# Splitting every tile of probabilities into two rounded parts, with one PSUM bank for the accumulator of values

## The chip, the cores and the metric

The kernel runs on one core of a Trainium2 chip. The metric is the device time of one execution in microseconds (us). The engines are named as in the profile: PE (matrix multiplication; PEld loads its weights), DVE (VectorE), ACT (ScalarE), POOL (GpSimd), SP (the queue that issues the DMAs). PSUM has eight banks of 128 x 512 float32 that PE writes and that ACT and DVE read.

## What is computed

One decoder layer for 1024 tokens of width 1024: attention beside a short convolution, then a gated feed-forward part, then a gated embedding. The change lies in the attention. For a block of 128 queries t (0 to 7) and a group g of four heads, three softmaxes are taken over different keys, and each is multiplied with its own values:

```
p_c = masked_softmax(s_c, cmp_end[None, :] <= tq[:, None])        # 63 compressed blocks
o_c = jnp.einsum('bgrqn,bngd->bqgrd', p_c, vcmp)
o_s = jnp.einsum('bgrqnk,bgqnkd->bqgrd', p_s, v_sel)              # selected keys (here all earlier ones)
o_w = jnp.einsum('bgrqk,bkgd->bqgrd', p_w, vwb)                   # a window of 512 keys
return gb[..., 0:1] * o_c + gb[..., 1:2] * o_s + gb[..., 2:3] * o_w
```

Behind it follow a norm over the heads and the product with w_o, whose rows feed the feed-forward part.

## The kernel before

Most products are taken in fp32r, a rounded float32, with both factors split into a rounded part and a remainder (high and low), so that three products stand for one. The values here hold high and low side by side in 128 columns, so a tile of probabilities needs two products: one for its high part `ph`, one for its low part `pl`.

The attention is written as 16 **units** (t, g), t from 7 down to 0, in slots: `at(slot, rank, fn)` files a piece of work under a slot and a rank, `run` carries them out in that order, and inside `tc.manual_schedule()` the instructions of each engine stand in the order in which they were recorded. While the scores of one unit are made (`score`: PE L666 to L669, DVE maximum L677, ACT exponential L683, DVE reciprocal L692, POOL scaling L694), `values` handles the tiles of the unit before it. For each tile of 128 keys:

- `turn`: PE transposes the four heads' probabilities into one PSUM bank (L719, tile `ba`);
- `keep`: ACT rounds the bank into `ph` (L731), and a slot part later DVE computes `pl` = bank minus `ph` (L735);
- `weigh`: PE multiplies `ph` and `pl` into the unit's accumulator, 128 x 512 (L753). The first `pl` of a unit is kept for last and closes the sum (L758).

`PLAIN[t]` says which tiles are not split: ACT copies the bank as it is into `pf` (L727), DVE does nothing, and PE multiplies `pf` in plain float32, which takes two passes in the profile. There are 28 such tiles of 148: 4 in each unit of t=7, 2 in t=3, 3 in t=2, 3 in t=1, 2 in t=0, none in t=6 to 4.

At a unit's end `close` empties the accumulator: ACT copies the lower half (`pvlo`, L767) and DVE adds it to the upper one (`oT`, L771, two instructions). For g=1, `norm_heads` follows (ACT `osq`, `oh`; DVE `ol` L810; PE sums L817; POOL power; PE spread L165 and ACT `rab`).

The accumulator's tile is `bv`, of which two may be open at once. The banks 4 to 7 serve the accumulator and the transposes, the others the scores. After the slots the last pieces and the rows of w_o (`row`, PE L101 to L103, then `row_rest` and `keep_form`) stand outside the manual order, and the scheduler of the language decides where they go. The rows of the second half of the tokens (`oh1`) depend on t=4 to 7 alone.

Of the kernel before, what the change touches and what calls it, by code (L numbers as in the profile page):

```python
# [10 lines left out]
P = 128  # L11
# [9 lines left out]
NCMP = 64  # L21
EPS = 1e-6
NEG = -1e30
PLAIN = (2, 2, 2, 1, 0, 0, 0, 2)

F32 = _mybir.dt.float32
F32R = _mybir.dt.float32r
# [14 lines left out]
X = dict(cmode=0, cd_r=5.98, ad_s=0, ad_r=5.27, nh_r=7, cl_s=0, cl_r=3.2, keep_s=1, keep_r=2,   # L42
         low_s=0, low_r=3.5, w_s=1, w_r=2.9, turn_r=3, sc_r=5, pk_s=0, pk_r=8, ex_s=1, ex_r=4, scl_s=1,
         scl_r=1, root_s=2, root_r=2.6, ap_s=2, ap_r=2.6, qs=5, qs_r=4.7, qt_s=2, qt_r=0.46, v0=2, off=0.0,
         ppf=6, pph=7, ppl=4, offu=4.46, v0r=-1, rt_l=3, fl_r=9, rv_r=1.79, rt_s=0, rt_r=2.6, pvb=2, trb=3,
         late=14, xa=3)


def _emit(nc, tc, d, out, tap=lambda *a: None):
# [4 lines left out]
    def S(shape, dt, tag, bufs=1):  # L54
        n_[0] += 1
        return sb.tile(list(shape), dt, tag=tag, bufs=bufs, name=f"{tag}_{n_[0]}")

    def PS(tag, bufs, cols=512, dt=F32):
        n_[0] += 1
        return psp.tile([P, cols], dt, tag=tag, bufs=bufs, name=f"{tag}_{n_[0]}")  # L60
# [4 lines left out]
    def psa(dt=F32):  # L65
        return PS("ba", 3, 512, dt)

    def psb():
        return PS("bb", 1)

    act, dve, pool, pe = nc.scalar, nc.vector, nc.gpsimd, nc.tensor
# [25 lines left out]
    def f32(ap):  # L97
        return ap.bitcast(F32)
# [21 lines left out]
    ident, ones, mhalf = small["ident"], small["ones"], small["mhalf"]  # L120
# [68 lines left out]
    with tc.manual_schedule():  # L189
# [5 lines left out]
        for k in range(KC):  # L195
# [3 lines left out]
            g = small["g_mix"][:, k:k + 1]  # L199
# [83 lines left out]
    for j in range(4):  # L283
# [17 lines left out]
        t = S([P, T], F32, "t4", 4)  # L301
# [17 lines left out]
        g = small["g_conv"][:, j:j + 1]  # L319
# [242 lines left out]
    vs, vw = va[:, :, 0:2], va[:, :, 2:4]  # L562
    vc = kx[:, NCMP + T + P:].rearrange("p (g c) -> p g c", g=2)
# [19 lines left out]
    def spans(t):  # L583
        nsel, w0 = (t + 1) * P, max(0, t - 4)
        return nsel, w0, (t + 1 - w0) * P

    def psa_(dt=F32):
        return psa(dt) if X["trb"] == 3 else PS("bt", X["trb"], 512, dt)
# [6 lines left out]
    def at(slot, rank, fn):  # L595
        todo.setdefault(slot, []).append((rank, len(todo.get(slot, ())), fn))

    stacks, probs, oT, sums, between = {}, {}, {}, {}, []
# [101 lines left out]
    def values(u, slot, ns):  # L700

        t, g = units[u]
        nsel, w0, nwin = spans(t)

        sel = [(vs[:, i, g], NCMP + i * P, P, False) for i in range(t + 1)]
        win = [(vw[:, w0 + i, g], NCMP + nsel + i * P, P, i % 4 < PLAIN[t]) for i in range(t + 1 - w0)]
        win.append((vc[:, g], 0, P, PLAIN[t] > 0))
        n = len(sel) + len(win)
        tiles = []
        while sel or win:  # L710
            tiles.append(win.pop(0) if win and (not sel or len(win) * (t + 1) > len(sel) * (t + 2 - w0)) and tiles
                         else sel.pop(0))
        st = {}

        def turn(i, s):
            v, pc, k, plain = tiles[i]
            pt = psa_()
            for r in range(4):
                pe.transpose(pt[0:k, r * P:(r + 1) * P], probs[u, r][:, pc:pc + k], ident)  # L719

            def keep():
                s1 = s + X["keep_s"]
                s2 = s1 + X["low_s"]
                s3 = s2 + X["w_s"]
                if plain:
                    pf = S([P, 512], F32, "pf", X["ppf"])[0:k]
                    act.copy(pf, pt[0:k])  # L727
                    at(s2, X["low_r"], lambda: at(s3, X["w_r"], lambda: weigh(i, s3, pf)))
                    return
                ph = S([P, 512], F32R, "ph", X["pph"])[0:k]  # L730
                act.copy(ph, pt[0:k])  # L731

                def low():
                    pl = S([P, 512], F32R, "pl", X["ppl"])[0:k]
                    dve.tensor_sub(pl, pt[0:k], f32(ph))  # L735
                    at(s3, X["w_r"], lambda: weigh(i, s3, ph, pl))
                at(s2, X["low_r"], low)
            at(s + X["keep_s"], X["keep_r"], keep)

        st["left"] = n  # L740

        def weigh(i, s, *ps):
            if "pv" not in st:
                st["pv"] = psb() if X["pvb"] == 1 else PS("bv", X["pvb"])
            pv, v = st["pv"], tiles[i][0]
            if len(ps) == 2 and "low" not in st:
                st["low"] = v, ps[1]
                ps = ps[0:1]
                first = True
            else:  # L750
                first = False
            for p in ps:
                pe.matmul(pv, f32(v) if tiles[i][3] else v, p, start=first, stop=False)  # L753
                if between:
                    between.pop(0)[1](s)
            st["left"] -= 1
            if st["left"] == 0:
                pe.matmul(pv, *st["low"], start=False, stop=True)  # L758
                at(s + X["cl_s"], X["cl_r"], lambda: close(s + X["cl_s"]))

        def close(s):
            pv = st["pv"]
            if g == 0:
                oT[t] = S([P, 4, P], F32, "oT", 2)
            if X["cmode"] == 0:
                lo = S([64, 512], F32, "pvlo", 1)
                act.copy(lo, pv[64:128])  # L767

                def add():
                    for par in range(2):  # L770
                        dve.tensor_tensor(oT[t][par * 64:par * 64 + 64, 2 * g:2 * g + 2],  # L771
                                          pv[0:64].rearrange("p (a b q) -> p b a q", a=2, b=2)[:, par],
                                          lo.rearrange("p (a b q) -> p b a q", a=2, b=2)[:, par], op=OP.add)
                    if g == 1:
                        at(s + 1, X["nh_r"], lambda: norm_heads(t, s + 1))
            else:
                parts = S([64, 1024], F32, "pvparts", 1)
                act.copy(parts[:, 512:1024], pv[64:128])
                at(s, X["cd_r"], lambda: dve.tensor_copy(parts[:, 0:512], pv[0:64]))
                pp = parts.rearrange("p (z a b q) -> p b z a q", z=2, a=2, b=2)  # L780

                def add():
                    for par in range(2):
                        dve.tensor_tensor(oT[t][par * 64:par * 64 + 64, 2 * g:2 * g + 2],
                                          pp[:, par, 0], pp[:, par, 1], op=OP.add)
# [63 lines left out]
    for u in range(len(units)):  # L849
# [3 lines left out]
        for i in range(slots[u]):  # L853
            r, part = (i, 0) if slots[u] == 4 else (i // 2, i % 2)
# [8 lines left out]
    def load_h0(m, hf, after=None):  # L863
        hins[m, hf] = S([P, 512], F32, "hin", 3)
        load(hins[m, hf], h0[m][:, hf * 512:(hf + 1) * 512], after)
# [8 lines left out]
    def keep_form(nm, k, y):  # L874
        i = FORMS.index(nm)
        where = i < 2, k
        if where not in forms_:
            forms_[where] = S([P, 2 if i < 2 else 5, 2, 512], F32R, f"forms{i < 2:d}{k}")
        hi, lo = (forms_[where][:, i if i < 2 else i - 2, z] for z in range(2))
        act.copy(hi, y)  # L880
        dve.tensor_sub(lo, y, f32(hi))  # L881
        form[nm][k] = hi, lo

    def row(m, hf, ps):
        s = slice(hf * 512, (hf + 1) * 512)
        wh, wl = (w[:, m % 2 * 4:m % 2 * 4 + 4] for w in wo[m // 2])
        for k in range(4):
            mm3(ps, wh[:, k], wl[:, k], oh[hf][:, k], ol[hf][:, k], k == 0, k == 3)
# [55 lines left out]
    for m in range(KC):  # L944
        load_h0(m, 1, late)
        if m % 2 == 0:
            wo[m // 2] = weights(d["wo_att"][m // 2], 1024, k=8, after=late)
        ps = PS("bh", 3)
        row(m, 1, ps)
        row_rest(m, 1, ps)  # L950
        keep_form("b11" if m < 4 else "b21", m % 4, yf[m, 1])
# [149 lines left out]
    with tc.manual_schedule():  # L1101
        for m in (0, 4, 1, 5):
            load_h0(m, 0)
        for n in range(-AHEAD, len(order)):
            if n >= 0:
                w, i = order[n]
# [87 lines left out]
    for k in range(KC):  # L1194
        hi = S([P, T], F32R, f"fh{k}")
        lo = S([P, T], F32R, f"fl{k}")
        g = small["g_ple"][:, k:k + 1]
# [22 lines left out]
    for m in range(KC):  # L1220
        wh, wl = wpg.pop() if wpg else weights(d["w_pg"][m], 1024, k=KC, by_act=True)
        for c, w in ((0, 512), (512, 512)) if m < KC - 1 else ((0, 512), (512, 256), (768, 256)):
            s = slice(c, c + w)
            ps = psa()[:, 0:w]
# [113 lines left out]
```

## Time and profile before

| | |
|---|---|
| median of 3 runs | 1489.8 us (1489.61 to 1490.05) |
| profiled execution | 1490.71 us, its span 1488.9 us |
| PE busy | 1433.8 us (96%) |
| DVE, ACT, POOL busy | 990.5, 584.2, 492.6 us |
| attention's units (values) | 358.5 to 612.2 us of the span |

Busy time of PE includes modelled ends of pipelined matmuls, so two neighbours overlap in it; the distance from one start to the next says what a matmul costs in a stream. The granted clock (PEclk) is 1.0 at 2.4 GHz and 0.5 at 1.2 GHz.

### The profile page before, as it was taken

The numbers are of one execution on the slowest core, as the hardware profiler recorded it, in microseconds if no ns is written. First come the engines' busy times: TensorE is split into PE (matmuls) and PEld (weight loads), VectorE is DVE, ScalarE is ACT, GpSimd is POOL, SyncE is SP. The second block draws the span as 40 slices with busy tenths as digits, with TensorE's granted clock in tenths as the row PEclk, the third lists the DMA queues.
The fourth block names the chain that finished last, engine by engine and source line by source line (L and its number), as shares of the span: only waits on it lengthen the run. The fifth ranks groups of instructions, "written<-read, shape, count | busy, mean of one in ns | idle before, by whom it ended". The sixth has DMA issues, their size and how long they took to land.

```text
span 1488.9 us, 19441 instructions
## 1 busy us (share of the span) xinstructions
PE 1433.8 (96%) x7207; PEld 1168.9 (79%) x7207; DVE 990.5 (67%) x1588; ACT 584.2 (39%) x1190; POOL 492.6 (33%) x467
## 2 busy tenths in 40 slices
PE   7999999998999999986999999999999999997998
PEld 6787898996777777765888888888888888876887
DVE  7645566546778888777777777877774344469533
ACT  4110131237868889653323333233335112125211
POOL 3221242465445558245223333333310000474000
PEclk9999999999989999997999999999999999999999
DMA  6221214300000002241222222222235123341211
GB/s 250 82 71 56 75 58 155 104 1 1 1 1 1 1 1 86 93 149 63 72 74 68 71 85 85 86 86 85 78 114 184 57 106 114 103 160 69 71 43 43
DMA packets 48190, 115.50 MB, mean 78 GB/s; under 512 B 5472, under 2 KB 8160, under 8 KB 48096
## 3 DMA queue, kind: packets, MB, share of 16 engines
q1 hardware_dynamic: 48096, 114.26, 22.8%
q8 instruction: 57, 0.93, 0.3%
q14 instruction: 37, 0.30, 0.1%
HBM read 90.12 MB, written 24.12 MB: 77 GB/s over the span
## 4 chain that ended last, share of the span: by engine, by line
PE 55%; DVE 6%; ACT 2%; issue 2%; DMA 1%; POOL 1%; SPq 0%; ACTq 0%; DVEq 0%; POOLq 0%
PE uy L1018 12%; PE uz L1018 8%; PE ux L1018 8%; PE ba L102 6%; PE ba L103 6%; PE ba L101 6%; PE bv L753 2%; PE ba L719 1%; DVE forms L881 1%; ACT P L683 1%; DVE h L1158 1%; PE b L666 1%; DVE t L1157 1%; PE b L101 1%; PE b L667 0%
## 5 line engine op out<-in xcount | busy, mean ns | idle before, releaser
L1018 PE MATMUL uy<-forms,wbh 128*128 128x512 f32 x528 | 166.6, 397 | 0.0
L694 POOL TENSOR_SCALAR P<-P,sc,consts 128x64 f32<-128x64 f32 (+8 forms) x192 | 129.2, 683 | 103.6 <-DVE sc L692 98.0
L984 POOL TENSOR_TENSOR wsum<-wup,wup 128x512 f32<-128x512 f32 x44 | 71.8, 1632 | 234.5 <-DMA wup<-in_w_up 201.6
L102 PE MATMUL ba<-actl,wh 128*128 128x512 f32 x352 | 138.1, 394 | 1.7 <-DVE actl L1140 1.6
L103 PE MATMUL ba<-acth,wl 128*128 128x512 f32 x352 | 137.5, 393 | 0.0
L101 PE MATMUL ba<-acth,wh 128*128 128x512 f32 x352 | 137.2, 393 | 0.0
L998 DVE TENSOR_TENSOR wbl<-wsum,wbh 128x512 fp32r<-128x512 f32 x88 | 79.8, 907 | 66.3 <-ACT wbh L997 66.3
L1018 PE MATMUL uz<-forms,wbh 128*128 128x512 f32 x352 | 112.8, 401 | 8.3 <-DVE forms L881 3.3
L1018 PE MATMUL ux<-forms,wbh 128*128 128x512 f32 x352 | 111.9, 399 | 9.2 <-ACT uv L1058 9.2
L677 DVE TENSOR_REDUCE nmax<-b 128x1 f32<-128x64 f32 (+8 forms) x192 | 96.7, 539 | 36.0 <-PE b L669 35.3
L1018 PEld LDWEIGHTS uy<-forms,wbh 128*128 128x128 f32 x528 | 100.3, 190 | 23.4
L683 ACT ACTIVATE P<-b,nmax 128x64 f32<-128x64 f32 (+8 forms) x192 | 108.9, 576 | 19.8 <-DVE sc L692 12.1
L143 DVE TENSOR_TENSOR wl<-wraw,wh 128x1024 fp32r<-128x1024 f32 (+3 forms) x93 | 92.2, 995 | 31.7 <-ACT wh L140 14.4
L1018 PE MATMUL uy<-forms,wbl 128*128 128x512 f32 x264 | 104.7, 396 | 0.0
L1154 DVE TENSOR_TENSOR h<-h,ba 128x512 f32<-128x512 f32 x64 | 43.8, 686 | 89.9 <-PE ba L103 89.8
L719 PE MATMUL ba<-consts,P 128*128 128x128 f32 x592 | 91.2, 278 | 5.3 <-DVE pl L735 2.5
L142 POOL TENSOR_SCALAR wh<-wraw 128x1024 fp32r<-128x1024 f32 (+2 forms) x37 | 47.9, 1298 | 133.3 <-PE b L102 46.1
L140 ACT CAST wh<-wraw 128x512 fp32r<-128x512 f32 (+2 forms) x56 | 35.3, 647 | 143.5 <-PE ba L102 119.6
L1160 POOL TENSOR_TENSOR h<-h,rfb 128x1024 f32<-128x1024 f32 x8 | 22.4, 2795 | 205.9 <-DVE h L1154 203.5
L719 PEld LDWEIGHTS ba<-consts,P 128*128 128x128 f32 x592 | 68.9, 143 | 23.9 <-issue 7.7
L1018 PEld LDWEIGHTS ux<-forms,wbh 128*128 128x128 f32 x352 | 67.1, 191 | 25.4 <-ACT uv L1058 9.6
L1018 PEld LDWEIGHTS uz<-forms,wbh 128*128 128x128 f32 x352 | 67.4, 192 | 24.8 <-DVE forms L881 3.6
(306 smaller groups left out, 3854.3 us busy)
## 6 DMA issues: line engine op xcount, KB each, us to landing
wup<-in_w_up SPq DMA_DIRECT2D x88, 256.0 KB, 4.1
aD<-ua SPq DMA_DIRECT2D x22, 512.0 KB, 2.9
t<-aD SPq DMA_DIRECT2D x22, 512.0 KB, 4.5
wraw<-in_w_down SPq DMA_DIRECT2D x32, 256.0 KB, 5.6
wraw<-in_wA SPq DMA_DIRECT2D x13, 512.0 KB, 3.6
hinc<-in_xT SPq DMA_DIRECT2D x16, 256.0 KB, 3.4
h<-t SPq DMA_DIRECT2D x16, 256.0 KB, 2.4
hin<-h SPq DMA_DIRECT2D x16, 256.0 KB, 4.2
```

Of the source, the lines that this page charges most:

```text
L101: pe.matmul(ps, ah, bh, start=first, stop=False)
L102: pe.matmul(ps, ah, bl, start=False, stop=False)
L103: pe.matmul(ps, al, bh, start=False, stop=last)
L142: pool.tensor_scalar(hi, raw, 1.0, 1.0, op0=OP.mult, op1=OP.mult)
L143: dve.tensor_sub(lo, raw, f32(hi))
L677: dve.tensor_reduce(nmax[:, b:b + 1], ps[:, o:o + w], axis=AX.X, op=OP.max, negate=True)
L683: act.activation(pr[:, pc:pc + w], ps[:, o:o + w], AF.Exp, bias=nmax[:, b:b + 1], accum_out=den[:, b:b + 1])
L694: pool.tensor_scalar(pr[:, pc:pc + w], pr[:, pc:pc + w], sc[:, b:b + 1], gates[:, t, hd * 3 + b:hd * 3 + b + 1], op0=OP.mult, op1=OP.mult)
L719: pe.transpose(pt[0:k, r * P:(r + 1) * P], probs[u, r][:, pc:pc + k], ident)
L984: pool.tensor_tensor(t, a, b, op=op)
L998: dve.tensor_sub(lo, y, f32(hi))
L1018: pe.matmul(ps, a[:, k], b, start=new and k == n_mm == 0, stop=k == 3 and n_mm == 2, skip_group_check=not new)
```

## The change

`PLAIN` goes away: all 148 tiles are split, `pf` is gone. The accumulator takes tile `bb`, of which one may be open (`pvb=1`), and the rows of w_o for the second half take their banks from `psa()` (tile `ba`) and not from `PS("bh", 3)`. Line numbers behind the first edit fall by one, behind `values` by six.

```diff
-PLAIN = (2, 2, 2, 1, 0, 0, 0, 2)
...
-         ppf=6, pph=7, ppl=4, offu=4.46, v0r=-1, rt_l=3, fl_r=9, rv_r=1.79, rt_s=0, rt_r=2.6, pvb=2, trb=3,
+         ppf=6, pph=7, ppl=4, offu=4.46, v0r=-1, rt_l=3, fl_r=9, rv_r=1.79, rt_s=0, rt_r=2.6, pvb=1, trb=3,
...
-        win = [(vw[:, w0 + i, g], NCMP + nsel + i * P, P, i % 4 < PLAIN[t]) for i in range(t + 1 - w0)]
-        win.append((vc[:, g], 0, P, PLAIN[t] > 0))
+        win = [(vw[:, w0 + i, g], NCMP + nsel + i * P) for i in range(t + 1 - w0)]
+        win.append((vc[:, g], 0))
...
-                if plain:
-                    pf = S([P, 512], F32, "pf", X["ppf"])[0:k]
-                    act.copy(pf, pt[0:k])
-                    at(s2, X["low_r"], lambda: at(s3, X["w_r"], lambda: weigh(i, s3, pf)))
-                    return
...
-                pe.matmul(pv, f32(v) if tiles[i][3] else v, p, start=first, stop=False)
+                pe.matmul(pv, v, p, start=first, stop=False)
...
-        ps = PS("bh", 3)
+        ps = psa()
         row(m, 1, ps)
```

Three places show what stands where. The first is PE at the first boundary between two units, t=7 g=0 to t=7 g=1: the last scores, the transposes of the next unit's second tile, and the first products of the next unit. Before:

```order
L669 MATMUL b_585_3575<-consts_61 128x128
L719 MATMUL ba_3587<-consts_61,P_3208 128x128 [waits DVE_49,PE_49]
L719 MATMUL ba_3587<-consts_61,P_3247 128x128
L719 MATMUL ba_3587<-consts_61,P_3319 128x128
L719 MATMUL ba_3587<-consts_61,P_3395 128x128
L753 MATMUL bv_3600<-ph_3553,vall_2784 128x512 [waits Activation_49]
L753 MATMUL bv_3600<-pf_3555,vall_2784 128x512
```

And of the changed kernel:

```order
L668 MATMUL b_590_3589<-consts_61 128x128
L718 MATMUL ba_3601<-consts_61,P_3208 128x128 [waits DVE_49,PE_49]
L718 MATMUL ba_3601<-consts_61,P_3247 128x128
L718 MATMUL ba_3601<-consts_61,P_3324 128x128
L718 MATMUL ba_3601<-consts_61,P_3401 128x128
L747 MATMUL bb_3614<-ph_3565,vall_2784 128x512 [waits DVE_49,Activation_49]
L747 MATMUL bb_3614<-ph_3567,vall_2784 128x512
L747 MATMUL bb_3614<-pl_3577,vall_2784 128x512
```

The order is the same but for one product more; the first product of the unit now waits for DVE too.

The second is DVE in t=1, from one `pl` to the next. Before:

```order
L735 TENSOR_TENSOR pl_6644<-ba_6615,ph_6641 128x512
L677 TENSOR_REDUCE nmax_6663<-b_1420_6655 128x1 x2
L679 TENSOR_SCALAR nmax_6663<-nmax_6663 128x1
L677 TENSOR_REDUCE nmax_6663<-b_1420_6655 128x1
L691 TENSOR_SCALAR den_6630<-den_6630 128x3
L692 RECIPROCAL sc_6631<-den_6630 128x3
L677 TENSOR_REDUCE nmax_6699<-b_1428_6691 128x1 x2
L679 TENSOR_SCALAR nmax_6699<-nmax_6699 128x1
L677 TENSOR_REDUCE nmax_6699<-b_1428_6691 128x1
L691 TENSOR_SCALAR den_6664<-den_6664 128x3
L692 RECIPROCAL sc_6665<-den_6664 128x3
L735 TENSOR_TENSOR pl_6717<-ba_6682,ph_6711 128x512
```

And of the changed kernel:

```order
L729 TENSOR_TENSOR pl_6678<-ba_6658,ph_6672 128x512
L676 TENSOR_REDUCE nmax_6697<-b_1435_6689 128x1 x2
L678 TENSOR_SCALAR nmax_6697<-nmax_6697 128x1
L676 TENSOR_REDUCE nmax_6697<-b_1435_6689 128x1
L690 TENSOR_SCALAR den_6654<-den_6654 128x3
L691 RECIPROCAL sc_6655<-den_6654 128x3
L729 TENSOR_TENSOR pl_6716<-ba_6683,ph_6709 128x512
```

A `pl` stands after each group of maxima now, not after every second one.

The third is PE at the end of the attention. Before, in the last unit but one (`bv_6752`), the whole row m=0 of w_o (`bh_6862`, 12 products) and the first product of row m=1 stand between two of the unit's products; three products of row m=1 in all stand ahead of the last unit's end:

```order
L719 MATMUL ba_6757<-consts_61,P_6533 128x128
L719 MATMUL ba_6757<-consts_61,P_6574 128x128
L753 MATMUL bv_6752<-pf_6750,vall_2784 128x512 [waits Activation_49]
L101 MATMUL bh_6862<-oh_437_3035,wh_6858 128x512
L102 MATMUL bh_6862<-ol_439_3037,wh_6858 128x512
L103 MATMUL bh_6862<-oh_437_3035,wl_6859 128x512
L101 MATMUL bh_6862<-oh_437_3035,wh_6858 128x512
```

Of the changed kernel, no row of the second half stands there. Four products of a row of the first half (`bp_7218`, which needs t=0) are among the last unit's, and from its closing product (L752) on PE has:

```order
L752 MATMUL bb_6885<-pl_6876,vall_2784 128x512
L101 MATMUL bp_7218<-ol_438_3036,wh_6942 128x512
L102 MATMUL bp_7218<-oh_436_3034,wl_6943 128x512
L811 MATMUL ba_6926<-consts_61,osq_6916 128x1 [waits Activation_49]
L811 MATMUL ba_6926<-consts_61,osq_6916 128x1 x3
L100 MATMUL bp_7218<-oh_436_3034,wh_6942 128x512 [waits Activation_49]
L164 MATMUL ba_6935<-consts_61,rar_6933 128x128 [waits PE_49,Pool_49]
L100 MATMUL ba_6946<-oh_437_3035,wh_6942 128x512
```

The rows of the second half (`ba_6946` is the first) stand behind the spread L164, which waits for the last unit's norm; before, they stood ahead of it and around it.

## Rows read from the trace of the kernel before

**Rows 1.** The page's busy time, share of the span and instructions of PE and DVE.
```profile
PE 1433.8 (96%) x7207; PEld 1168.9 (79%) x7207; DVE 990.5 (67%) x1588; ACT 584.2 (39%) x1190; POOL 492.6 (33%) x467
```
**Rows 2.** By stretch: length; PE, PEld, DVE, ACT, POOL busy (count); PEclk; DMA share, GB/s.
```profile
358.50:402.30 43.80, 43.74 (x268) 32.04 (x267) 30.91 (x63) 34.47 (x81) 20.38 (x27) 1.00 0.01 1
402.30:430.30 28.00, 25.39 (x142) 19.94 (x141) 19.60 (x43) 18.57 (x46) 10.86 (x14) 0.82 0.00 1
430.30:523.50 93.20, 91.67 (x621) 73.36 (x620) 82.29 (x187) 80.96 (x206) 48.00 (x68) 1.00 0.00 1
523.50:556.20 32.70, 31.55 (x203) 23.06 (x202) 26.56 (x67) 28.83 (x86) 18.43 (x30) 1.00 0.00 1
556.20:599.40 43.20, 42.31 (x286) 32.36 (x285) 35.59 (x114) 39.76 (x141) 34.04 (x57) 1.00 0.21 74
```
**Rows 3.** Timeline of PE in t=7: start, duration, engine, line, operation [idle before].
```profile
362.80 1.02 PE L753 MATMUL bv<-pf,vall 128*128 128x512 f32 x2
363.65 0.60 PE L719 MATMUL ba<-consts,P 128*128 128x128 f32 x4
...
365.72 0.40 PE L753 MATMUL bv<-ph,vall 128*128 128x512 f32 x1
365.95 0.40 PE L753 MATMUL bv<-pl,vall 128*128 128x512 f32 x1
366.19 0.60 PE L719 MATMUL ba<-consts,P 128*128 128x128 f32 x4
```
**Rows 4.** Groups by line, 358.5 to 613 us: count, busy us, mean ns, idle before.
```profile
L735 DVE TENSOR_TENSOR pl<-ba,ph 128x512 fp32r<-128x512 f32 x119 | 78.0, 677 | 8.4 <-ACT ph L731 8.1
L731 ACT CAST ph<-ba 128x512 fp32r<-128x512 f32 x119 | 68.5, 591 | 15.0 <-PE ba L719 14.8
L727 ACT COPY pf<-ba 128x512 f32<-128x512 f32 x27 | 16.1, 595 | 2.7 <-PE ba L719 2.4
```
**Rows 5.** Timeline at three boundaries: the first, t=6 g=0 to g=1, t=4 g=0 to g=1.
```profile
379.68 0.39 PE L758 MATMUL bv<-pl,vall 128*128 128x512 f32 x1
380.19 0.67 DVE L735 TENSOR_TENSOR pl<-ba,ph 128x512 fp32r<-128x512 f32 x1
380.78 0.83 DVE L771 TENSOR_TENSOR oT<-bv,pvlo 64x256 f32<-64x256 f32 x2
381.50 0.47 PE L753 MATMUL bv<-ph,vall 128*128 128x512 f32 x1
...
431.50 0.84 DVE L771 TENSOR_TENSOR oT<-bv,pvlo 64x256 f32<-64x256 f32 x2
431.75 0.71 PE L753 MATMUL bv<-ph,vall 128*128 128x512 f32 x2
...
508.36 0.71 PE L753 MATMUL bv<-ph,vall 128*128 128x512 f32 x2
508.53 0.84 DVE L771 TENSOR_TENSOR oT<-bv,pvlo 64x256 f32<-64x256 f32 x2
```
**Rows 6.** Timeline of DVE and PE in t=6 g=0.
```profile
410.00 1.89 DVE L810 SCALAR_TENSOR_TENSOR ol<-oT,consts,oh 128x128 fp32r<-128x128 f32 x4
412.63 1.09 PE L719 MATMUL ba<-consts,P 128*128 128x128 f32 x4 [2.46 <-DVE pl L735]
```
**Rows 7.** Timeline of PE and ACT at the end of the attention.
```profile
602.48 0.79 PE L101 MATMUL bh<-oh,wh 128*128 128x512 f32 x1
607.41 0.58 ACT L767 COPY pvlo<-bv 64x512 f32<-64x512 f32 x1 [2.26 <-PE bv L758]
611.43 0.79 PE L758 MATMUL bv<-pl,vall 128*128 128x512 f32 x1
616.67 0.38 PE L165 MATMUL ba<-consts,rar 128*128 128x128 f32 x2
```
**Rows 8.** The chain of work behind the rows of w_o, in order of time.
```profile
628.07 1.98 DMA hD<-hm
632.83 4.27 DMA wup<-in_w_up
```

More of the change, by code (lines that the diff above doesn't have):

```diff
@@ L703, in values @@
         nsel, w0, nwin = spans(t)
-        sel = [(vs[:, i, g], NCMP + i * P, P, False) for i in range(t + 1)]
-        win = [(vw[:, w0 + i, g], NCMP + nsel + i * P, P, i % 4 < PLAIN[t]) for i in range(t + 1 - w0)]
-        win.append((vc[:, g], 0, P, PLAIN[t] > 0))
+        sel = [(vs[:, i, g], NCMP + i * P) for i in range(t + 1)]
+        win = [(vw[:, w0 + i, g], NCMP + nsel + i * P) for i in range(t + 1 - w0)]
+        win.append((vc[:, g], 0))
         n = len(sel) + len(win)
@@ L715, in turn @@
         def turn(i, s):
-            v, pc, k, plain = tiles[i]
+            v, pc = tiles[i]
             pt = psa_()
             for r in range(4):
-                pe.transpose(pt[0:k, r * P:(r + 1) * P], probs[u, r][:, pc:pc + k], ident)
+                pe.transpose(pt[:, r * P:(r + 1) * P], probs[u, r][:, pc:pc + P], ident)
             def keep():
@@ L724, in keep @@
                 s3 = s2 + X["w_s"]
-                if plain:
-                    pf = S([P, 512], F32, "pf", X["ppf"])[0:k]
-                    act.copy(pf, pt[0:k])
-                    at(s2, X["low_r"], lambda: at(s3, X["w_r"], lambda: weigh(i, s3, pf)))
-                    return
-                ph = S([P, 512], F32R, "ph", X["pph"])[0:k]
-                act.copy(ph, pt[0:k])
+                ph = S([P, 512], F32R, "ph", X["pph"])
+                act.copy(ph, pt)
                 def low():
-                    pl = S([P, 512], F32R, "pl", X["ppl"])[0:k]
-                    dve.tensor_sub(pl, pt[0:k], f32(ph))
+                    pl = S([P, 512], F32R, "pl", X["ppl"])
+                    dve.tensor_sub(pl, pt, f32(ph))
                     at(s3, X["w_r"], lambda: weigh(i, s3, ph, pl))
@@ L745, in weigh @@
             pv, v = st["pv"], tiles[i][0]
-            if len(ps) == 2 and "low" not in st:
+            if "low" not in st:
                 st["low"] = v, ps[1]
```

## The prediction

> **What bounds the kernel now.** I read the page first: PE is busy for 96% of the span and DVE for 67% [rows 1], so PE's time counts wherever no other engine is as full. The attention is such a stretch and the only one in which the change removes work, so I cut it at the ends of its units [rows 2]. The reader should compare three columns. For t=7 (358.5 to 402.3 us) PE is full and DVE has 12.9 of 43.8 us free. For t=6 g=1 to t=4 PE leaves 1.5 of 93.2 us, DVE 10.9. For t=2 and 1 (556.2 to 599.4) PE has 42.3 of 43.2 us, ACT 39.8 and DVE 35.6: three engines are nearly full, and what one of them gives back the next may keep.
>
> **What a tile gains on PE.** In the stream of t=7 a plain tile starts at 362.80 and the next instruction at 363.65, so it costs 0.85 us; `ph` and `pl` of a split tile run from 365.72 to 366.19, 0.47 us, 0.23 us each [rows 3]. The change gives back 0.38 us for each of 28 tiles, 10.6 us in all: 3.0 in t=7, 1.5 in t=3, 2.3 in t=2 and 2.3 in t=1, 1.5 in t=0. If PE alone set the time, that would be the result.
>
> **What a tile costs elsewhere.** ACT empties the bank either way, 595 ns for a copy and 591 for a rounding: nothing. DVE gets 28 subtractions of 677 ns [rows 4], 19.0 us, and the bank stays taken until they are done. In t=7 DVE's free 12.9 us cover 8 x 0.68 = 5.4. In t=2 and 1 twelve more make 8.1 us, and 35.6 + 8.1 = 43.7 is more than the stretch has (43.2), while PE would need 42.3 - 4.6 = 37.7. There DVE becomes the bound, and the 4.6 us do not come back. If DVE ran without a hole, the stretch would lose 0.5 us; if half of its present 7.6 idle us stayed (waits for ACT's rounding, for scores, for the close), it would lose 4.3; if DVE found room after all, it would win 4.6. I take a loss of 1.0, since DVE is fed by two engines that both have less work ahead of it than before.
>
> **What one bank costs.** With two accumulators, PE starts the next unit while ACT and DVE still empty the last one; with one, its first product waits for the second `oT` addition, as the rows of PE's order show. Behind that product stand, in PE's queue, all further products, transposes and scores of the unit, and DVE's maxima wait for those. The price is how much later `oT` ends than the product starts today. At the first boundary that is 381.61 against 381.50, but a further `pl` now stands ahead of `oT` on DVE, so 0.11 + 0.68 = 0.79. Inside t=6 to 4 no tile changes, and the five boundaries (t=6 g=1 to t=4 g=1) read directly: the first 431.50 + 0.84 - 431.75 = 0.59, the last 508.53 + 0.84 - 508.36 = 1.01, the mean of the five 0.86, so 4.3 us [rows 5]. A PE that comes later finds some of its present waits answered; it has 1.5 us of them there [rows 2], and I count 1.0 back: +3.3. At least 2.8 stays if all of the 1.5 goes, at most 4.3.
>
> The boundary into t=6 g=0 I price at nothing: 9 us behind it PE idles 2.46 us for a `pl` that stands on DVE behind four `ol` (1.89 us) [rows 6], so a PE that comes 0.7 us later there only waits less. If that cover goes, it costs those 0.7. For t=3 two boundaries at 0.86 stand against 1.5 gained: +0.2 (between -1.5 and +1). The boundaries inside t=2 and 1 lie in the stretch that DVE sets and are not counted again.
>
> A rule of the Trainium skill speaks against this edit: Perfetto Trace Analysis, section Optimizing Tensor Performance (Matmuls), wants independent groups of matmuls to rotate through different PSUM banks, so that emptying one overlaps the products of the next. Taken at its word, each boundary would lay the whole emptying bare; rows 5 show that transposes and scores of the next unit fill part of it, which is why I count 0.86.
>
> **What the scheduler moved.** Before, 15 products of w_o's rows m=0 and 1 stand ahead of the last unit's closing product: from 602.48 on they fill PE while ACT is behind, and the rest runs right behind the close [rows 7]. In the changed order none of them does, and behind the close PE meets sums, one product that waits for `oh` and a spread that waits for the whole norm, before the first of eight rows. Before, that norm took from the end of the close (612.22) to the spread (616.67), 4.4 us, all under rows. Now PE has three products and the sums in it, about 1.5 us, and idles 2.9. The 15 products come later, 15 x 0.23 = 3.5. On the other side the units end earlier without the row between them: ACT waited 2.26 us for PE there [rows 7]; a `pl` of 0.68 now stands in its place, and I count 1.0. Seven products of `bp` are done early, 1.6 us, of which I count half, because what follows hangs on the rows' results: the chain goes from them to the store of `hm`, behind it in SP's queue to the load of `wup` [rows 8], and on. Sum: 3.5 + 2.9 - 1.0 - 0.8 = +4.6, between 0 (nothing idle, all credits) and 6.4 (no credit). The banks of the rows change name only; the tiles are as many and as large: nothing, and a wait for a bank would show at a row's first product.
>
> **The sum.** t=7: -3.0 + 0.8 = -2.2. t=6 to 4: +3.3. t=3: +0.2. t=2 and 1: +1.0. End with t=0: +4.6. Together +6.9 us. The profiled execution took 1490.7 (span 1488.9 and 1.8 around it), 0.9 above the median of 1489.8; from the median I forecast 1496.7, slower by 0.5%. The bounds added one way give 1485 and 1504.
>
> **The rivals.** *DVE has room* (faster). In t=3 to 0 the subtractions slip into DVE's holes and PE keeps its 7.6 us, boundaries of t=3 to 0 included. Then -2.2 + 3.3 - 7.6, and the end without t=0's share costs 4.6 - 1.2 = 3.4 since ACT and DVE are ready sooner: -3.1, 1486.7. It is decided by whether 8.1 us fit into 7.6 idle ones in t=2 and 1; that ACT and DVE drained at the end (ACT's 2.26 us) speaks for it, the sum 43.7 of 43.2 against. Chance 0.16.
>
> *The clock falls at the end* (slower still). In t=6 g=0 the granted clock is 0.82 over 28.0 us [rows 2]; between its two levels, 2.4 and 1.2 GHz, that is 10.1 us at the lower one, which costs about 5.0 us, and it comes right at the idle 2.46 us of PE [rows 6]. The wait that I expect behind the last unit is as long. If the clock falls there too, the rows of w_o pay for it: 1501.7. Against it: it may also happen that the fall in t=6 is missing, which would give 1491.7. Chance 0.13 for the fall, 0.08 for the missing one.
>
> *The rule holds in full.* If no transposes or scores could run meanwhile, each of 15 boundaries would cost the whole time from the end of the close (380.07) to the end of `oT` (381.61), 1.54 us [rows 5], 23.1 in place of the 6.8 counted: 1513. The order leaves sixteen instructions between, so 0.03.
>
> The change does what it says; both its edits are seen in the order.
>
> **How the numbers follow.** My forecast has 0.60 and by itself spans 1492.8 to 1501. The range of 8 in 10 leaves out the rule in full, the upper part of the fallen clock and the better half of DVE's room: 1488 to 1504. A difference below 0.2% (3.0 us) can hardly be told from none. Faster by more takes the better 0.11 of DVE's room and of sums near it; the rest of that case and most of the missing fall lie within 0.2%, 0.12; slower 0.77.
>
> **What would show it.** Windows over t=7 should shrink by about 2 us. At each boundary in t=6 to 4 the first product should wait for DVE `oT`, 0.6 to 1.0 us each. In t=2 and 1 DVE should be busy for over 95% and PE wait for `pl`. Behind the last close PE should show a wait of 2 to 3 us ending at `oh` or at POOL's power, and the first row of w_o should start at least 2 us later against the close than before. I am wrong if the boundaries show no wait (then the bank was no matter), if PE stays the fullest engine in t=2 and 1, or if the start of the feed-forward part does not move with the rows.

## The result and the profile after

The changed kernel took 1502.36 us (median of 4, 1501.74 to 1503.19), the kernel before 1489.92 beside it (4 runs, 1489.61 to 1490.59): slower by 0.83%, 12.4 us (ratio 1.0083, interval 1.0066 to 1.0101). The profiled execution took 1502.69, its span 1500.9, so 12.0 us more than the span of before. On the page the busy times look like those of [rows 1]:

```profile
PE 1433.2 (95%) x7207; PEld 1174.6 (78%) x7207; DVE 996.3 (66%) x1616; ACT 584.9 (39%) x1190; POOL 489.2 (33%) x467
```

DVE has its 28 subtractions more (1616 against 1588 instructions); PE has as many records as before, since a plain tile left two of them [rows 3], as a split one does. What changed is seen only by stretch. The same five stretches as in [rows 2], each from the end of a unit's closing product to that of another, with the same columns:

```profile
360.79:401.81 41.02, 40.41 (x267) 31.96 (x266) 34.70 (x70) 33.29 (x78) 19.44 (x25) 1.00 0.00 1
401.81:425.70 23.89, 20.99 (x142) 16.57 (x141) 19.70 (x44) 18.68 (x46) 10.85 (x14) 1.00 0.01 1
425.70:521.13 95.43, 91.15 (x620) 73.23 (x619) 82.64 (x186) 81.34 (x206) 47.80 (x68) 1.00 0.00 1
521.13:553.52 32.39, 29.92 (x203) 23.22 (x202) 28.61 (x71) 28.93 (x86) 17.91 (x30) 1.00 0.00 1
553.52:600.75 47.23, 43.24 (x287) 36.55 (x285) 41.36 (x125) 40.08 (x141) 34.41 (x57) 0.89 0.19 68
```

The first row shrank. The second shrank by 4 us and its clock is 1.00 where it was 0.82: the fall of the clock in t=6 g=0 is missing here. The third and the last grew. In the last, t=2 and 1, DVE has 41.4 of 47.2 us, 88%, and the clock is 0.89 where it was 1.00.

The table below holds all profiled executions, before's and the experiments' too, worked out from the ends of the closing products (L758, L752 after). "Start" is the first product with probabilities, a unit pair runs from close to close, and "tail" reaches from the last close to the feed-forward product that waits 2.14 us for DVE `uw`: 695.98 before, 708.02 after. Behind it there is nothing to find, 792.9 us in both.

| us | start | t=7 | t=6 | t=5, 4 | t=3 | t=2 | t=1 | t=0 | tail | at 1.2 GHz in t=6 / t=2 to 0 |
|---|---|---|---|---|---|---|---|---|---|---|
| before | 358.7 | 43.7 | 47.4 | 73.8 | 32.7 | 24.2 | 19.1 | 12.8 | 83.8 | 10.2 / 0 |
| after | 360.8 | 41.0 | 43.7 | 75.6 | 32.4 | 23.1 | 24.2 | 14.6 | 92.7 | 0 / 17.1 |
| e1 one bank | 357.4 | 43.9 | 43.9 | 76.3 | 32.9 | 24.1 | 21.6 | 13.1 | 81.4 | 0 / 0 |
| e2 rows | 362.7 | 43.6 | 44.6 | 73.8 | 32.7 | 24.1 | 19.1 | 11.6 | 91.5 | 3.4 / 0 |
| e3 split t=3 to 0, rows | 360.8 | 43.6 | 44.3 | 73.8 | 32.3 | 24.0 | 24.5 | 15.0 | 93.1 | 3.4 / 17.1 |
| e4 as e3, one bank | 359.8 | 43.9 | 43.9 | 76.2 | 32.4 | 24.1 | 25.0 | 15.0 | 92.9 | 0 / 17.1 |
| e5 split t=7, one bank | 361.0 | 41.0 | 43.7 | 75.6 | 32.8 | 24.2 | 21.6 | 13.1 | 81.9 | 0 / 0 |
| e6 split t=1, rows | 361.0 | 43.6 | 44.6 | 73.8 | 32.7 | 24.3 | 22.1 | 11.7 | 91.4 | 3.4 / 6.8 |
| e7 all but t=1 | 359.7 | 41.0 | 45.4 | 75.6 | 32.4 | 23.1 | 24.9 | 14.5 | 92.7 | 3.4 / 13.7 |
| e8 split t=7, 3, one bank | 360.3 | 41.0 | 43.8 | 75.6 | 32.4 | 24.1 | 21.3 | 13.1 | 82.4 | 0 / 0 |
| e9 all but t=2 to 0 | 361.3 | 41.0 | 43.8 | 75.6 | 32.4 | 24.1 | 20.2 | 11.6 | 91.7 | 0 / 0 |
| e10 as e9, subtractions | 360.2 | 41.1 | 45.3 | 75.6 | 32.4 | 24.3 | 24.2 | 13.3 | 93.2 | 3.4 / 3.4 |
| e11 as e9, two products | 359.2 | 41.0 | 46.9 | 75.6 | 32.4 | 23.3 | 19.1 | 14.1 | 91.7 | 6.8 / 6.8 |
| e12 more products | 360.1 | 41.1 | 45.4 | 75.6 | 32.5 | 23.9 | 23.2 | 15.4 | 92.7 | 3.4 / 10.2 |

The first two lines differ by -2.6 in t=7, -3.7 in t=6, +1.8 in t=5 and 4, -0.3 in t=3, +4.0 in t=2 and 1, +1.8 in t=0 and +8.9 in the tail; the start is 2.1 later. What time at 1.2 GHz costs can be read in t=6, where e9, e10 and e11 have the same instructions: with 0, 3.4 and 6.8 us of it they take 43.8, 45.3 and 46.9 us, so 1 us at the lower clock costs about 0.45. The start moves between 357.4 and 362.7 in kernels that are the same up to there, so I do not put it down to the change.

### The profile page after: what moved, and what is told of

Read it like the earlier page. It is cut to its first block, busy times and chain, and to the rows that moved or that the text cites. A ratio compares the mean times of both kernels' runs of the same rounds, so it can differ in the third digit from the quotient of the medians.

```text
span 1500.9 us, 19477 instructions
## 1 busy us (share of the span) xinstructions
PE 1433.2 (95%) x7207; PEld 1174.6 (78%) x7207; DVE 996.3 (66%) x1616; ACT 584.9 (39%) x1190; POOL 489.2 (33%) x467
## 4 chain that ended last, share of the span: by engine, by line
PE 53%; DVE 7%; ACT 2%; issue 2%; DMA 1%; POOL 1%; SPq 0%; DVEq 0%; ACTq 0%; POOLq 0%
PE uy L1012 12%; PE uz L1012 8%; PE ux L1012 7%; PE ba L101 7%; PE ba L102 7%; PE ba L100 7%; DVE forms L875 1%; PE bb L747 1%; PE ba L718 1%; DVE fl L1193 1%; DVE h L1152 1%; DVE t L1151 1%; DMA t<-aD 1%; ACT P L682 1%; DVE wl L142 1%
## 5 line engine op out<-in xcount | busy, mean ns | idle before, releaser
L978 POOL TENSOR_TENSOR wsum<-wup,wup 128x512 f32<-128x512 f32 x44 | 67.0, 1525 | 237.5 <-DMA wup<-in_w_up 218.8
L992 DVE TENSOR_TENSOR wbl<-wsum,wbh 128x512 fp32r<-128x512 f32 x88 | 75.2, 854 | 67.1 <-ACT wbh L991 64.0
L142 DVE TENSOR_TENSOR wl<-wraw,wh 128x1024 fp32r<-128x1024 f32 (+3 forms) x93 | 91.3, 986 | 32.7 <-ACT wh L139 16.0
L1148 DVE TENSOR_TENSOR h<-h,ba 128x512 f32<-128x512 f32 x64 | 43.8, 686 | 90.4 <-PE ba L102 90.3
L729 DVE TENSOR_TENSOR pl<-ba,ph 128x512 fp32r<-128x512 f32 x148 | 96.1, 677 | 7.4 <-ACT ph L725 6.6
L725 ACT CAST ph<-ba 128x512 fp32r<-128x512 f32 x148 | 84.7, 590 | 19.7 <-PE ba L718 18.9
L141 POOL TENSOR_SCALAR wh<-wraw 128x1024 fp32r<-128x1024 f32 (+2 forms) x37 | 46.9, 1269 | 133.9 <-PE b L101 46.6
```

Source lines behind the costliest of these rows:

```text
L142: dve.tensor_sub(lo, raw, f32(hi))
L725: act.copy(ph, pt)
L729: dve.tensor_sub(pl, pt, f32(ph))
```

## The experiments

Times are medians; differences are against the kernel before beside them (1489.61, then 1490.27, then 1490.57 us). Executions of one kernel spread with their mean granted clock: of the kernel before one took 1485.2 us at 0.989 and another 1493.1 at 0.984. Where a table row and a median disagree by a few us, this is why; the profiled execution of e1, for one, is its fastest, 1486.45 at 0.992, the others had 0.985 to 0.988.

**The parts alone.** e1 takes one bank, e2 the other tile for the rows, e3 the splitting of t=3 to 0 together with the rows, e4 all but the splitting of t=7. The edits here and below are against the kernel before, shortened.

```diff
e1, e4:
-         ... pvb=2, trb=3,
+         ... pvb=1, trb=3,
e2, e3, e4:
-        ps = PS("bh", 3)
+        ps = psa()
e3, e4:
-PLAIN = (2, 2, 2, 1, 0, 0, 0, 2)
+PLAIN = (0, 0, 0, 0, 0, 0, 0, 2)
```

> The kernel before with the one bank alone: the tiles of probabilities stay as they were, and so do the rows of w_o. Theory A (the wait at each boundary is what the bank costs): the first product of each unit waits 0.6 to 1.0 us for the second oT addition; 13 of the 15 boundaries (those into t=6 g=0 and behind the last row excepted) at 0.86 are 11.2 us, of which about 4 are absorbed by waits that PE has today: +7, 1497. Theory B (the bank costs little, what cost 12 us were falls of the granted clock at places where PE idled behind the split tiles of t=2 to 0): the boundaries of t=6 to 4 cost 4 us, and if the fall inside t=6 g=0 is missing here as it was in the changed kernel, 5 come back: 1490 within 2; no new time at the lower clock between 556 and 640 us of the span.

Measured: 1493.60, +4.0 (1.0030, 1.0017 to 1.0042). The boundaries do wait: over t=6 g=1 to t=4 PE waits five times for `oT`, 3.9 us, and t=5 and 4 are 2.5 us longer. Theory A has the place right and is 3 us too dear. Theory B's 4 us for these five boundaries is right, and the fall in t=6 is missing as it asked, but its 1490 is outside the interval. It left out t=1, which is 2.5 us longer with one bank. The accumulator need not stay in one bank, though. In the programs as built, in e1 and e4 it lies in bank 4 at each of these boundaries, while where t=7 is split it lies in bank 5 in t=6 and in bank 4 from t=5 on. There the wait at the change of bank is missing, as in the changed kernel at 446.57 (timeline of PE and DVE around three boundaries):

```profile
427.85 0.47 PE L747 MATMUL bb<-ph,vall 128*128 128x512 f32 x1 [0.49 <-DVE oT L765]
...
446.57 0.71 PE L747 MATMUL bb<-ph,vall 128*128 128x512 f32 x2
446.69 0.84 DVE L765 TENSOR_TENSOR oT<-bb,pvlo 64x256 f32<-64x256 f32 x2
...
467.92 0.47 PE L747 MATMUL bb<-ph,vall 128*128 128x512 f32 x1 [0.79 <-DVE oT L765]
```

The second product starts before the first addition of `oT` ends. That is one boundary of five, and 0.7 us: t=5 and 4 take 75.6 with the change of bank, 76.3 without.

> The kernel before, and only the tile of w_o's rows is taken from the other tag. Theory A as on record (the banks change name only; the rows move behind the last close because of the split tiles and the one bank): the program up to the last unit is the same, and the time is 1490. Rival A2 (the tag alone moves the rows: a tile of the shared tag can be given out only when the scores and transposes no longer ask for it): the 15 products stand behind the last close, PE idles 2 to 3 us there, and the time is +4.6 as priced on record, 1494.5. Theory B: if the idle time there also makes the granted clock fall over the feed-forward's start, another 3 to 5 us, 1498.

Measured: 1498.68, +9.1 (1.0054, 1.0040 to 1.0067). The name of the tile is the dearest of the three edits. Rival A2 holds in its mechanism, with half of the price: nothing else is changed, and the rows stand behind the last close, as the timeline of PE shows:

```profile
611.40 0.79 PE L758 MATMUL bv<-pl,vall 128*128 128x512 f32 x1
612.03 0.38 PE L165 MATMUL ba<-consts,rar 128*128 128x128 f32 x2
612.16 0.48 PE L101 MATMUL bp<-oh,wh 128*128 128x512 f32 x1
...
614.40 1.05 PE L817 MATMUL ba<-consts,osq 128*128 128x1 f32 x8 [0.59 <-ACT osq L801]
615.32 0.48 PE L101 MATMUL bp<-oh,wh 128*128 128x512 f32 x1
616.38 0.49 PE L165 MATMUL ba<-consts,rar 128*128 128x128 f32 x2 [0.59 <-POOL rar L825]
616.63 0.48 PE L101 MATMUL ba<-oh,wh 128*128 128x512 f32 x1
...
638.80 0.40 PE L103 MATMUL ba<-oh,wl 128*128 128x512 f32 x1
```

The kernel before has a row at once behind the closing product of [rows 7], and its last row ends earlier:

```profile
612.06 0.39 PE L101 MATMUL bh<-oh,wh 128*128 128x512 f32 x1
...
631.79 0.40 PE L103 MATMUL bh<-oh,wl 128*128 128x512 f32 x1
```

In e2 the first row starts 4.4 us behind the close (612.19) and the last one ends 27.0 us behind it (639.20), before 20.0 (632.19 against 612.22). The 15 products that stood ahead of the close are 3.5 of these 7.0, the norm that no row covers is the rest. PE does not stand still much in the 4.4 us, since seven products of `bp` run there; but they win nothing, for later PE waits 1.54 us for POOL `rfr`, and then 9.1 us for ACT `uv` as before (9.2). The tail grows by 7.7, t=0 gives back 1.2. No clock falls between the units and the rows, so B's further 3 to 5 us are not there. Why the tile decides is argued only: tiles of `ba` are handed out in turn with those of transposes, sums and spreads, `bh` had its own turn.

> Splitting in t=3 to 0 (20 tiles), the rows of w_o from the other tag, two banks for the accumulator, and t=7 as before. Theory A: t=7 to 4 unchanged against the kernel before, t=3 gains 1.5, t=2 and 1 lose 1.0, the end loses 4.6: +4.1, 1494. Rival (DVE has room): t=3 to 0 keep 7.6 us and only the end costs 3.4: 1486. Theory B (clock): in t=1 PE waits for pl and the granted clock falls there; the fall of 10.2 us at the lower clock in t=1 costs 5.1, and the feed-forward's start another 4: 1499.

> As the run before (splitting in t=3 to 0, rows from the other tag) and one bank for the accumulator: all of the change but the splitting of t=7. Theory A: the bank adds 3.3 in t=6 to 4 and 1.7 in t=3, little in t=2 to 0: 5 us over the run before; and the changed kernel, which splits t=7 too, is 2.2 faster than this: 1504. Theory B: where the clock falls in t=6 g=0 decides; if it falls there (the PE idles there as before), the time is 1506, if not, 1501; the splitting of t=7 changes the time by its own 3 us only.

Measured: e3 1503.02, +13.4 (1.0087, 1.0073 to 1.0101); e4 1506.88, +17.3 (1.0113, 1.0099 to 1.0127). The bank adds 3.9 to e3 as it did to the kernel before. Against e2, e3 loses 4.3, and the table says where: t=3 gains 0.4, t=2 nothing, t=1 and 0 lose 8.8, with 17.1 us at the lower clock that e2 has not. Theory A has no place for that; theory B has, so the next runs go there. No theory has the size: e3 was put at 1494 (A), 1499 (B) and 1486 (the rival), and e4, whose profile has no fall in t=6, at 1504 (A) and, for that case, at 1501 (B).

**Which tiles.** e5 and e8 look for what is worth keeping, e6 and e7 for the tiles behind the loss in t=1.

```diff
-PLAIN = (2, 2, 2, 1, 0, 0, 0, 2)
+PLAIN = (2, 2, 2, 1, 0, 0, 0, 0)     e5, with pvb=1
+PLAIN = (2, 0, 2, 1, 0, 0, 0, 2)     e6, with psa()
+PLAIN = (0, 2, 0, 0, 0, 0, 0, 0)     e7, with pvb=1 and psa()
+PLAIN = (2, 2, 2, 0, 0, 0, 0, 0)     e8, with pvb=1
```

> The kernel before with one bank and with the eight plain tiles of t=7 split; t=3 to 0 and the rows of w_o stay as before. Against the one bank alone (3.9 us over the kernel before): by the term on record t=7 gives back 2.2, and the time is 1.7 over the kernel before. Rival: the two units give back more, as the difference between the run with everything but t=7 (+17) and the whole change (+12.4) says, 4.5: then the time is that of the kernel before, within 1.

> A version that could be best by the sums so far: one bank, t=7 and t=3 split, t=2 to 0 plain, the rows of w_o on their own tag. By the terms on record: bank 3.9, t=7 -2.2 (or -4.5 by the rival of e5), t=3 -1.5: +0.2 or -2.1 against the kernel before. Rival: t=3 gives nothing, since what PE gains there it waits for ACT in t=2 (the run that split t=3 to 0 showed 0.4 only): then it is the time of the run that split t=7 alone.

Measured: e5 1489.38, -0.9 (0.9999, 0.9988 to 1.0009); e8 1487.50, -2.8 (0.9980, 0.9972 to 0.9989). The rival of e5 holds: splitting t=7 is worth 4 to 5 us, 2.9 in its own units (43.9 to 41.0) and 0.7 by the change of bank. e8 is the only one of these versions that beats the kernel before; its forecast of +0.2 or -2.1 was near. That it needs the one bank was not tried. Its rows for t=6 g=0 and for t=2 and 1, to be set against [rows 2]:

```profile
401.27:425.20 23.93, 21.02 (x142) 16.57 (x141) 19.68 (x44) 18.67 (x46) 10.87 (x14) 1.00 0.01 1
...
553.06:598.46 45.40, 44.03 (x293) 33.65 (x292) 36.20 (x115) 39.89 (x141) 34.33 (x57) 1.00 0.20 70
```

Its gain goes with a steadier clock: all 11 of its executions had 0.989 or 0.990, the 23 of before 0.983 to 0.990, and in the profile t=6 is 3.6 us shorter without the fall. Why the clock holds there is not settled.

> The rows of w_o from the other tag and, of all plain tiles, only the six of t=1 split; two banks. It is to be set against the rows alone (9.1 over the kernel before). Theory C (splitting t=1 by itself opens the waits of PE for ph and pl there, and the granted clock falls behind them): a fall of about 10 us at the lower clock between 585 and 600 us of the span, more behind it, +5: 14 over the kernel before. Rival D (DVE is late in t=1 only because the tiles of t=2 and 3 were split too and it cannot catch up): no fall, the time is 8 to 10 over the kernel before.

> The whole change but for the six tiles of t=1, which stay plain. Theory C: no fall of the clock between 585 and 600 us, and the time is 5 us or more below the changed kernel: 7 over the kernel before. Rival D: PE still waits in t=1 for a DVE that is late from t=2, the fall stays, and the time is that of the changed kernel, 12 over the kernel before.

Measured: e6 1500.69, +10.4 (1.0068, 1.0054 to 1.0082); e7 1503.31, +13.0 (1.0088, 1.0073 to 1.0103). Theory C falls: with t=1 plain, t=1 is as slow as in the whole change (24.9) and the time is the same. Splitting t=1 alone costs t=1 3.0 us, though, and e6 has a fall of 6.8 us there, from 589.3 on, for 1.3 us more than e2 by the medians. So D is not all either: t=1 pays for its own splitting and for what comes late from t=2.

**DVE's part and PE's part.** All four are the changed kernel but for the 16 tiles of t=2 to 0 that were plain before.

```diff
e9: PLAIN = (2, 2, 2, 0, 0, 0, 0, 0), pvb=1, psa()
e10: as e9, and for a plain tile, ahead of its product
+                        pl = S([P, 512], F32R, "pl", X["ppl"])[0:k]
+                        dve.tensor_sub(pl, pt[0:k], pf)
e11: as e9, for these tiles
-                    act.copy(pf, pt[0:k])
-                    ... weigh(i, s3, pf)
+                    act.copy(ph, pt[0:k])
+                    ... weigh(i, s3, ph, ph)
-                pe.matmul(pv, f32(v) if tiles[i][3] else v, p, start=first, stop=False)
+                pe.matmul(pv, v, p, start=first, stop=False)
e12: the changed kernel, for these tiles
-                    ... weigh(i, s3, ph, pl)
+                    ... weigh(i, s3, ph, pl, pl)
```

> The whole change but for t=2 to 0, whose 16 plain tiles stay plain: t=7 and t=3 split, one bank, rows of w_o from the other tag. Sum of the runs so far: rows +8 to 9, bank +4, t=7 -4, t=3 -3: 5 to 6 over the kernel before, and no time at the lower clock between 580 and 625 us of the span. If instead it comes within 2 us of the changed kernel (+12.4), the loss is not in the tiles of t=2 to 0.

> As the run before, and DVE subtracts for each of the 16 plain tiles of t=2 to 0 although nothing reads the result: DVE's part of the splitting without PE's gain; the products stay plain. Theory L (DVE's 10.8 us of subtractions, and the banks kept for them, make PE wait): 7 or more over the run with plain t=2 to 0, and the clock falls at 585. Theory K (PE with less work idles more, and the clock falls for that): within 2 of it, no fall.

> As the run with plain t=2 to 0, but its 16 tiles are multiplied as split ones (two products with the rounded part, in place of one plain product) and nothing is subtracted: PE's part of the splitting without DVE's; the low parts of these tiles are left out. Theory L: PE keeps its 16 x 0.38 = 6.1 us or the part of it that ACT lets it have: 2 to 6 below the run with plain t=2 to 0. Theory K: the clock falls at 585 and eats it: 2 to 6 above.

> The whole change, and in the 16 tiles of t=2 to 0 that it splits the product with the low part is made twice, 16 x 0.23 = 3.7 us more on PE (the output takes these low parts double). Theory K: a busier PE keeps its clock and the time falls below that of the changed kernel by 2 or more. Theory L: DVE and ACT set the pace, the product fills a wait, and the time is that of the changed kernel or up to 3.7 more, with the falls as they were.

Measured: e9 1497.79, +7.2 (1.0060, 1.0036 to 1.0083); e10 1503.38, +12.8 (1.0092, 1.0074 to 1.0110); e11 1495.81, +5.2 (1.0041, 1.0027 to 1.0054); e12 1501.87, +11.3 (1.0090, 1.0067 to 1.0112). e9 is a little above its sum (5 to 6) and has no fall in t=2 to 0, as forecast. The subtractions alone, with no product changed, bring the time of the whole change: t=2 to 0 grow from 55.9 us (e9) to 61.8, which is what the changed kernel has, and the median by 5.6 us, though the intervals of e9 and e10 still touch. Only 3.4 us of that run are at the lower clock there, against 17.1, so a loss of this size does not need such falls. PE's part alone saves 2.0 of the medians, less than the intervals tell apart, and not the 6.1 that its products would give: in e11 t=2 and 1 are 1.9 us shorter than in e9, but t=0 is 2.5 longer, with 6.8 us at the lower clock and nothing subtracted. And 16 products more cost nothing by the medians (e12), in a profile with 6.9 us less at the lower clock than the changed kernel's. Theory L is nearer: its 7 us were too much, and its fall of the clock is short and late (590). The times that K gave came in none of the three, but e11 shows that a fall can come without the subtractions and cost what PE gained. The windows over t=1 in e9, e10 and the changed kernel, in this order:

```profile
578.19:598.38 20.19, 18.54 (x128) 14.17 (x127) 15.77 (x63) 17.89 (x68) 14.74 (x28) 1.00 0.04 14
```
```profile
578.50:602.70 24.20, 20.87 (x128) 15.40 (x126) 19.79 (x68) 17.91 (x68) 15.18 (x29) 0.93 0.00 1
```
```profile
576.59:600.75 24.16, 21.08 (x129) 18.23 (x128) 20.66 (x69) 17.90 (x67) 16.23 (x28) 0.79 0.07 23
```

ACT has the same 17.9 us in all three; PE is not full in any. DVE goes from 15.8 to 19.8 and 20.7, and the stretch grows by 4.0 us each time, though DVE is only 82 to 86% busy in it. The chain of work of the changed kernel tells how that can be (start, length, what; the kernel's line numbers are those behind the change):

```profile
576.78 0.08 DVE sc L691
576.86 1.18 DVE pl L729 x2
578.03 0.33 DVE oT L765
...
578.83 0.89 DVE nmax L676 x3
579.71 0.08 DVE sc L691
579.80 0.58 DVE pl L729
580.37 0.94 DVE wl L142
...
582.20 1.17 DVE wl L142
...
584.31 0.58 DVE pl L729
...
585.22 1.13 DVE wl L142
...
586.91 1.15 DVE ol L804 x4
588.06 0.61 DVE pl L729
588.67 0.14 issue
588.81 1.09 PE ba L718 x4
```

From 575.91 to 588.67 the chain does not leave DVE but for moments. Three `wl` (subtractions that split later weights, 1.34 us each), four `ol` and the `pl` stand in one queue with the maxima and reciprocals that ACT, POOL and PE wait for. Busy times from the start of t=1 g=0 to its last transposes, and in the same stretch of e9 below; DVE runs five `pl` and three `wl` in the one, two `pl`, one `wl` and the end of another in the other:

```profile
576.59:588.81 12.22, 9.14 (x61) 7.67 (x59) 12.14 (x34) 10.03 (x36) 10.79 (x15) 0.84 0.14 45
```
```profile
578.19:587.31 9.12, 8.05 (x60) 6.25 (x59) 8.52 (x27) 9.00 (x32) 8.12 (x13) 1.00 0.01 3
```

DVE is full to 99% in the one and to 93% in the other, where the chain goes through PE and ACT as well; the run costs 3.1 us. Behind it the bound is another. The rest of t=1 and the second part of t=0 in the changed kernel, and that part of t=0 in e9:

```profile
588.81:600.75 11.94, 11.94 (x69) 10.56 (x70) 8.52 (x37) 7.87 (x31) 5.45 (x13) 0.73 0.00 0
606.71:615.30 8.59, 8.59 (x36) 7.36 (x37) 5.21 (x13) 3.10 (x7) 0.55 (x1) 0.68 0.00 0
```
```profile
604.20:610.04 5.84, 5.84 (x32) 4.05 (x32) 2.12 (x6) 2.78 (x6) 0.60 (x2) 1.00 0.00 0
```

PE shows no pause in these parts of the changed kernel, and 11.9 us of them are at the lower clock. By the 0.45 of t=6 these cost an estimated 5.4 us, about as much as the whole loss of t=2 to 0. By this estimate the splitting costs the changed kernel the run on DVE, gains on PE behind it, and loses that gain to the lower clock. Whether the run brings the falls about is not shown: e10 has the run and one short fall behind it, e11 has a fall in t=0 without the subtractions. The Trainium skill, Perfetto Trace Analysis, section Identifying the Most-Contended Engine, goes by occupancy for the vector engine, and for PE not by the busy time of matmuls but, beside another measure, by that of weight loads. By this it would name DVE over t=2 and 1 already, with 88% against 77% for PEld (36.55 of 47.23), and the trace agrees for the run above; it doesn't tell the run from what follows it, where PE is full.

## Why the prediction was right or wrong

The sign and the range held; the time, 5.7 us too low, came about otherwise than forecast. That it lies in the range is in part luck: by the profiled executions the end and t=2 and 1 cost 9.1 us more than forecast, and the fall in t=6, which was missing, gave about 4.6 back. With that fall the time would have been an estimated 1507, above the range. By the prediction's own steps:

| step | forecast | profile |
|---|---|---|
| t=7 | -2.2 | -2.6 |
| five boundaries, t=6 g=1 to t=4 | +3.3 | +2.2 (93.2 to 95.4) |
| boundary into t=6 g=0 | 0 | +0.5 (-4.1 + 4.6), an estimate |
| t=6 g=0, missing fall (a rival) | 0 | -4.6, an estimate |
| t=3 | +0.2 | -0.3 |
| t=2 and 1 | +1.0 | +4.0 |
| end with t=0 | +4.6 | +10.7 |
| start of the attention | 0 | +2.1 |
| sum | +6.9 | +12.0 |

**t=7, t=3 and the boundaries** were right in mechanism. The waits for `oT` were forecast at 0.6 to 1.0 us each and are 0.49, 0.79, 0.79 and 0.91, with none at the fifth, where the bank changes; so the five cost 2.2 us, below the 2.8 that the prediction called the least. By the medians t=7 is worth 4.9 (e5 against e1) and not 2.2, in part by that change of bank. The fall in t=6, 10.2 us at the lower clock and by the 0.45 about 4.6 us, is missing, the rival that had 0.08. What was said of PE's 2.46 us idle there [rows 6] gave no reason for it: after, PE idles 2.14 at the same place, and the clock stays.

The rule of the Trainium skill that the prediction weighed (Perfetto Trace Analysis, Optimizing Tensor Performance, Matmuls) is borne out in its direction by the change of bank at 446.57, where the wait is gone. Its price is 0.5 to 0.9 us of waiting, near what rows 5 gave, not 1.54.

**The end** is the step that failed, in cause and in size. The prediction said of the rows that "the banks of the rows change name only" and put down nothing, and gave the moved products to the scheduler without asking which edit moved them. e2 shows that this name alone moves them, for 6.5 of the 10.7 us (tail +7.7, t=0 -1.2). The sum for it, 3.5 + 2.9 - 1.0 - 0.8, has the products (3.5) and the credit of t=0 (1.2) right and the norm (3.5) nearly. The credit of 0.8 for early products of `bp` was wrong, since a wait for the rows' norm (1.54 us in e2, 1.32 after) and the wait for `uv` stand behind it. The other 4 us are t=0 (+3.0 against e2) and the tail (+1.3), where the clock falls at 619 for 3.4 us while the rows run. Of the 3.0 in t=0, 2.8 lie in the part where PE is full (8.6 us; 5.8 in e9), of which 5.5 us are at the lower clock, an estimated 2.5 us; four early products of `bp` (0.9) stand there too. The timeline of PE shows both the wait and the fall:

```profile
615.14 0.39 PE L101 MATMUL bp<-ol,wh 128*128 128x512 f32 x1
615.37 0.40 PE L102 MATMUL bp<-oh,wl 128*128 128x512 f32 x1
617.52 1.05 PE L811 MATMUL ba<-consts,osq 128*128 128x1 f32 x8 [1.75 <-ACT osq L795]
618.43 0.48 PE L100 MATMUL bp<-oh,wh 128*128 128x512 f32 x1
619.50 0.80 PE L164 MATMUL ba<-consts,rar 128*128 128x128 f32 x2 [0.59 <-POOL rar L819]
619.95 0.77 PE L100 MATMUL ba<-oh,wh 128*128 128x512 f32 x1
620.52 0.63 PE L101 MATMUL ba<-ol,wh 128*128 128x512 f32 x1
620.95 0.63 PE L102 MATMUL ba<-oh,wl 128*128 128x512 f32 x1
```

The waits end at `osq` (not `oh`) and at POOL's power, 1.75 and 0.59 us, 2.3 of the forecast 2 to 3. The first row starts 4.65 us behind the close (615.30). From 620.52 rows stand 0.43 us apart, 0.23 in e2.

**t=2 and 1**: the engine was right for the run, the sum was not. 43.7 us of work in 43.2 let DVE become the bound by a hair, with +4.3 as the worst. Taken against e9, which has the bank but not the split tiles, t=2 to 0 lose 5.9, and the bank itself costs t=1 1.1 (2.2 to 2.5 in e1, e5 and e8). DVE is not full over the stretch, 88% where over 95% was forecast, because its work comes in a run: the `pl` meet `wl` and `ol` in t=1 g=0 and everything behind waits for that run. A sum over 43 us cannot show it. PE, with 92% (43.24 of 47.23), stays the fullest, which the prediction had named as a sign of being wrong, and from t=2 to 0 it waits 1.6 us for `pl` against 3.1 for ACT's `ph`. The rival that DVE has room is refuted by e3 and e10. The one that the clock falls at the end came true in part, earlier than it said (584.9 in t=1); that its 1501.7 is nearest to the result is luck, since it took the rest of the sum as forecast. In e10 the loss is as large with 3.4 us at the lower clock, but in the changed kernel PE is full while the clock is low. What its t=1 and 0 would take without the falls is an estimate only, since none of the runs had its waits without them.

By the medians the parts add up: rows 9.1, bank 4.0, t=7 -4.9 (e5 against e1), t=3 -1.9 (e8 against e5), t=2 to 0 +5.2 (whole change against e9), together 11.5 of 12.4. The intervals of e9 and of the whole change touch, so the last of these is the least sure.

## What to carry to other kernels

The tag from which a product takes its bank can decide where its instructions stand, here for 9 us: build each such edit alone and look where the instructions go before it is priced at nothing. Whether an engine has room for more work is read in the few us where its work comes in a run, ahead of what the others wait for, and not from its share of a long stretch. Here the same splitting gained 2.6 us where DVE had room in its queue (t=7) and lost 5.9 where it met other work (t=2 to 0, the lower clock behind it included), and the version that splits only t=7 and t=3 and leaves the rows where they were is the fastest of those built.

## What was not expected of the hardware

The granted clock does not follow from PE's pauses as the trace shows them. Ahead of the attention, before and after have the same instructions on PE and the same last pauses: 0.95 us (up to 354.13 before, 354.64 after) and 0.80 us (up to 355.25 and 355.77). Before, the clock stays at 2.4 GHz; after, it is at 1.2 from 356.2 to 359.6. The windows of before and of after:

```profile
350.00:360.00 10.00, 7.86 (x49) 5.64 (x50) 7.53 (x18) 8.65 (x23) 7.91 (x10) 1.00 0.00 0
```
```profile
350.00:360.00 10.00, 7.61 (x38) 5.42 (x37) 6.94 (x15) 7.96 (x22) 7.49 (x11) 0.83 0.00 0
```

Of the fourteen profiled executions six have a fall there and eight have none, and in t=6 the time at 1.2 GHz is 0, 3.4, 6.8 or 10.2 us. So a kernel like this gains or loses some us for a reason that its own code does not show. e8 has the fall ahead of the attention too and none in t=6; why its mean clock is so steady, 0.989 or 0.990 each time, stays open.
